# The second half's rows are normed beside units 8 to 10 instead of beside three recurrences

## The chip, the cores and the metric

The kernel runs on one core of a Trainium2 chip. What counts is the device time of one execution in microseconds (us). A profiled execution gives, beside its time, a record of every instruction on the engines PE (matrix products; PEld is its weight loads), DVE, ACT and POOL, and of SP, which issues most of the transfers (DMAs).

## The reference

One inference step of a decoder with two layers: 2048 prompt tokens and 8 x 4 sample tokens of width 1024. Layer 0 (even) has a gated recurrence (HGRN2) and attention with forgetting in parallel; layer 1 (odd) is a gated linear attention (GLA) with four heads. Each layer norms its input rows, multiplies them by an input matrix, mixes, gates, and adds the product with an output matrix to its input. Cut to the part that the change touches:

```
def run_trunk(x, ...):
    # layer 0
    x = x + even_mixer(rmsnorm(x, norm_even[0]), ...)
    # layer 1
    x = x + odd_mixer(rmsnorm(x, norm_odd[0]), ...)
    return rmsnorm(x, final_norm), ...

def odd_mixer(h, w_in, w_gate, b_gate, gla_gain, w_out, gla_s0):
    proj = h @ w_in
    q, k, v, g, r = _split(proj, [C_KEY_WIDTH, C_KEY_WIDTH, C_VAL_WIDTH, C_VAL_WIDTH, C_GATE_RANK])
    log_f = jax.nn.log_sigmoid((r @ w_gate + b_gate)) / GLA_GATE_NORMALIZER
    o, s = gated_linear_chunked(q, k, v, log_f, gla_s0)       # per head, 128 keys x 256 values
    o = head_rmsnorm(o, gla_gain) * jax.nn.silu(g)
    return o @ w_out, s
```

What the change moves is `rmsnorm(x, norm_odd[0])` for the second half of the prompt rows.

## The kernel before, in words

The prompt is worked on in two halves of 1024 tokens; the first half carries the 32 sample tokens as well. The normed, transposed input of a half lies in one tile, `act`, as a high and a low half-precision part, and every product with a weight matrix is made of three matmuls (`mm3`, L603 to L607). There is one `act` tile, so the second half's rows can go into it only when the first half's products are done.

The products come in *units*, numbered in one list: units 0 to 3 are the even layer's output projection of the first half, 4 to 7 that of the second; 8 to 19 are the odd layer's input projections of the first half, three for each head (v, then q and k, then the gate g); 20 to 31 the same for the second half; 32 to 39 the odd layer's output projections. `dense(a, b)` makes units a to b-1 and, beside each, starts the weight load of the unit three further on (L334, on SP) and the split of the weights of the unit two further on into two parts (L352 to L360, on ACT, DVE and POOL). A unit of v (`proj_tm`) goes through 8 groups of 128 rows and one of the samples, a unit of q and k or of g (`proj_fm`) through six pieces of 352 columns; each fills a PSUM bank of the tag "pj", of which there are three, and ACT (and DVE) empties it (L1884 for v, L1938 and L1943 for q and k, L662 to L664 for g).

A head's recurrence is `lin_attn`: products of q and k (`gd`, then the levels `gl`, L738) whose results are copied by mask (L684, L753), rescaling of q, k and the decay (L771 to L773), the samples' states (`stS`, L823 to L828), and the chunks' products (`st`, `o`). `recur(hf, h, a)` runs it beside units a to a+2.

Rows are normed by `norm_store` in one step per 128 rows: it loads the rows (L540, SP) from the array `x1d` into a tile `x1r`, squares and sums them (L546, ACT), makes the reciprocal root (L410 on DVE, L412 on POOL), multiplies by the gain (L548, POOL), writes the high part (L553, ACT) and the low part (L554, DVE), and stores both (L555, SP) in the array `xs`. A step norms one row tile and finishes the one before it. For the second half (`hf == 1`) the tiles are two buffers of the tag "yr"; the load of a step is one step ahead. In the code loads stand behind the last transposing DMA (`self.last_turn`, L538 to L540, order of issue only). `norm_fetch` brings `xs` into `act` with transposing DMAs (L574, SP).

The order of the work: `mux(a, ta, b, tb)` writes out two streams of steps so that each is at the same share of its cost (`ta`, `tb`). A step of `prep(1)` counts 1000, a group of a unit of v 2640, a piece of the other units 3592. What is written out is only the priority: a scheduler that runs a simulated timeline at build time (`schedule_with_timeline_sim=True`, L2192) puts the instructions of each engine in an order, which then is fixed. `issue_after` adds edges to it.

Of the kernel before, what the change touches and what calls it, by code (L numbers as in the profile page):

```python
# [76 lines left out]
def mux(a, ta, b, tb):  # L77

    pa = pb = 0.0
    la = lb = True  # L80
    while la or lb:
        if la and (not lb or pa * tb <= pb * ta):
            c = next(a, None)
            la = c is not None
            pa += c or 0
        else:
            c = next(b, None)
            lb = c is not None
            pb += c or 0
        if c:  # L90
            yield c
# [20 lines left out]
def drain(g):  # L112
    for _ in g:
        pass
# [11 lines left out]
class Kern:  # L126
# [1847 lines left out]
    def phase_odd(self):  # L1974
# [4 lines left out]
        with pool("act2", side="right") as ap, pool("w2", side="right") as w0, pool("yr2", side="right") as y0, \  # L1979
# [34 lines left out]
            def dense(a, b):  # L2014
                return self.staged(units, a, b)

            def recur(hf, h, a):
                return mux(lins[hf](h), LIN_O[hf], dense(a, a + 3), 66000.0)

            def three(hf, a):  # L2020
                for h in range(3):
                    yield from recur(hf, h, a + 3 * h)

            def fetched(u):
                units[u][0][0]()
                self.early.add(u)
# [57 lines left out]
            def prep(hf):  # L2084

                def tiles(c0):
                    p, tag = (wp, "v8") if hf == 0 and c0 // P % 2 else (wpool, "yr")
                    t = p.tile([P, KT, 256], F32, tag=tag, name=f"x1r{hf}{c0}").rearrange("p k t -> p (k t)")
                    return t[:, :D], t[:, D:].bitcast(F16).rearrange("p (x d) -> p x d", x=2)

                return self.norm_store(wp, hf, tiles, grow, 1 + (hf == 0))
# [1 line left out]
            drain(mux(prep(0), 11500.0, dense(4, 7), 63000.0))  # L2093
            self.norm_fetch(act, 0, dense(7, 8))
            fetched(11)
            drain(dense(8, 11))
            drain(mux(prep(1), 10000.0, three(0, 11), 240000.0))
            fetched(23)
            self.norm_fetch(act, 1)
            drain(recur(0, 3, 20))  # L2100
# [95 lines left out]
```

## Time and profile before

| | |
|---|---|
| median of three runs | 2337.07 us |
| lowest and highest of them | 2333.03 and 2337.43 us |
| the profiled execution | 2338.06 us |
| its span, first to last instruction | 2336.2 us |
| mean granted clock of PE in it | 0.991 |
| busy: PE, PEld, DVE, ACT, POOL | 96%, 69%, 62%, 46%, 33% of the span |

The profile's times are counted from the span's start. Units 8 to 10 lie from 1458 to 1528, the recurrences of heads 0, 1 and 2 of the first half from 1528 to 1619, to 1714 and to 1811. Busy time of a stretch, waits (who waited for whom, by the semaphore that came last), the chain of waits that ended last, and the instructions in order of time are views of the same trace. Durations of matmuls overlap, since they are pipelined.

### The profile page before, as it was taken

The page shows a single profiled execution, that of the slowest core. Times are in us where ns is not written, and L with a number is a line of the kernel's source. Part 1 is how long each engine was busy: PE and PEld are TensorE (multiplying, and loading weights), DVE is VectorE, ACT ScalarE, POOL GpSimd, SP SyncE. Part 2 cuts the span into 40 slices and gives each one's busy share as a digit, 9 for nine tenths or more (in the row PEclk, how much of TensorE's full clock was granted, in tenths as well). Part 3 has the DMA queues.
Part 4 walks back from the last instruction along what each step waited for, and adds up shares of the span by engine and source line. Part 5 has one row for each costly group of instructions (what it writes and reads, how often), then busy time and mean ns, then how long its engine had stood idle before and what let it go on. Part 6 is the DMA issues. An engine that isn't in the chain of part 4 may idle for free.

```text
span 2336.2 us, 58122 instructions
## 1 busy us (share of the span) xinstructions
PE 2250.3 (96%) x23060; PEld 1604.1 (69%) x23060; DVE 1448.0 (62%) x3313; ACT 1076.2 (46%) x2360; POOL 768.7 (33%) x818
## 2 busy tenths in 40 slices
PE   7999999999999989999999999999899999999998
PEld 5667667864655876665545888777677666666887
DVE  7766577537655748667767445366675655557554
ACT  6434344333333326555656543546545545545343
POOL 2333324112212214223335445144552432322232
PEclk9999999999999999999999999999999999999999
DMA  7232334765441278877882968523233431115554
GB/s 201 66 93 67 94 106 152 182 170 138 147 136 43 89 178 268 247 234 221 271 249 73 341 198 261 141 84 119 75 113 86 126 104 58 46 58 163 167 188 150
DMA packets 375665, 344.87 MB, mean 148 GB/s; under 512 B 107633, under 2 KB 322994, under 8 KB 375394
## 3 DMA queue, kind: packets, MB, share of 16 engines
q1 hardware_dynamic: 373250, 334.54, 47.8%
q0 software_dynamic: 2144, 6.62, 0.8%
q8 instruction: 181, 2.97, 0.5%
q14 instruction: 90, 0.74, 0.1%
HBM read 244.54 MB, written 79.63 MB: 139 GB/s over the span
## 4 chain that ended last, share of the span: by engine, by line
PE 78%; DVE 8%; DMA 4%; ACT 3%; issue 2%; POOL 2%; SPq 2%; POOLq 0%; DVEq 0%; ACTq 0%
PE pt_o L605 4%; PE pt_o L607 4%; PE pt_o L606 4%; PE pkt L1546 2%; PE pt L1427 2%; PE pt_Cv L605 2%; PE pt_Cv L606 2%; PE pt_Cv L607 2%; PE sc L1605 1%; PE pv L1684 1%; PE pf_Ag L607 1%; PE pf_Ag L606 1%; PE pf_Ag L605 1%; PE pf_Bq L607 1%; PE pf_Bq L606 1%
## 5 line engine op out<-in xcount | busy, mean ns | idle before, releaser
L605 PE MATMUL pt_o<-w_o,act 128*128 128x256 f16 x1024 | 279.7, 273 | 2.3 <-ACT sg1C L662 2.3
L607 PE MATMUL pt_o<-w_o,act 128*128 128x256 f16 x1024 | 279.6, 273 | 0.9 <-POOL act L1785 0.9
L606 PE MATMUL pt_o<-w_o,act 128*128 128x256 f16 x1024 | 279.6, 273 | 0.0
L605 PEld LDWEIGHTS <-act 128*128 128x128 f16 x2304 | 226.7, 98 | 37.4 <-issue 4.1
L606 PEld LDWEIGHTS <-act 128*128 128x128 f16 x2304 | 226.8, 98 | 32.9 <-issue 3.6
L607 PEld LDWEIGHTS <-act 128*128 128x128 f16 x2304 | 226.8, 98 | 31.4 <-issue 1.9
L606 PE MATMUL pt_Cv<-w_Cv,act 128*128 128x256 f16 (+1 forms) x512 | 141.3, 276 | 0.0
L605 PE MATMUL pt_Cv<-w_Cv,act 128*128 128x256 f16 (+1 forms) x512 | 141.3, 276 | 0.0
L607 PE MATMUL pt_Cv<-w_Cv,act 128*128 128x256 f16 (+1 forms) x512 | 141.2, 276 | 0.0
L772 POOL TENSOR_TENSOR kA<-kA,fA 128x512 f32<-128x512 f32 (+1 forms) x56 | 77.9, 1392 | 186.2 <-PE gl_A L738 140.2
L772 POOL TENSOR_TENSOR kC<-kC,fC 128x512 f32<-128x512 f32 (+1 forms) x56 | 83.9, 1498 | 153.9 <-PE gl_C L738 107.8
L1407 POOL TENSOR_SCALAR L<-L,nm 128x512 f32<-128x512 f32 (+3 forms) x160 | 99.5, 638 | 104.6 <-DVE nm L1403 44.5
L1399 ACT ACTIVATE L<-L,nm,kc 128x512 f32<-128x512 f32 (+3 forms) x160 | 118.2, 741 | 28.9 <-DVE nm L1397 27.6
L1434 ACT ACTIVATE th<-pt 128x512 f16<-128x512 f32 (+3 forms) x159 | 81.6, 528 | 85.1 <-PE pt L1427 82.0
L1435 DVE TENSOR_TENSOR tl<-pt,th 128x512 f16<-128x512 f32 (+3 forms) x159 | 95.0, 608 | 20.3 <-ACT th L1434 18.3
L1427 PE MATMUL pt<-ident,L 128*128 128x128 f32 x544 | 90.6, 278 | 2.1 <-DVE tl L1435 1.1
L1546 PEld LDWEIGHTS pkt<-ident,pgcache_fox_k 128*128 128x128 f32 x512 | 58.9, 142 | 42.9 <-issue 25.6
L1427 PEld LDWEIGHTS pt<-ident,L 128*128 128x128 f32 x544 | 66.4, 142 | 25.8 <-DVE tl L1435 6.2
L1884 ACT ACTIVATE vC<-pt_Cv,kc 128x512 f32<-128x512 f32 (+1 forms) x40 | 23.9, 598 | 130.4 <-PE pt_Cv L607 130.4
L1546 PE MATMUL pkt<-ident,pgcache_fox_k 128*128 128x128 f32 x512 | 77.6, 279 | 6.1 <-DMA pgcache_fox_k<-in_cache_fox_k 1.8
L1374 POOL TENSOR_TENSOR cm<-cb,caus 128x128 f32<-128x128 f32 x64 | 29.1, 456 | 132.1 <-DVE mx L1391 114.4
L605 PE MATMUL pt_Bk<-w_Bk,act 128*128 128x256 f16 x256 | 70.5, 276 | 2.1 <-DVE Bvs L1049 1.8
(959 smaller groups left out, 6750.7 us busy)
## 6 DMA issues: line engine op xcount, KB each, us to landing
pgcache_fox_k<-in_cache_fox_k SPq DMA_DIRECT2D x128, 256.0 KB, 4.2
pgcache_fox_v<-in_cache_fox_v SPq DMA_DIRECT2D x128, 256.0 KB, 4.0
yr<-yT SPq DMA_DIRECT2D x16, 1024.0 KB, 8.1
x1d<-xo SPq DMA_DIRECT2D x44, 256.0 KB, 3.9
wr_Aqf<-in_w_in_even SPq DMA_DIRECT2D x64, 128.0 KB, 3.2
wr_o<-in_w_out_even SPq DMA_DIRECT2D x32, 256.0 KB, 5.3
xo<-in_x_prompt SPq DMA_DIRECT2D x32, 256.0 KB, 5.3
wr_Cv<-in_w_in_odd SPq DMA_DIRECT2D x32, 256.0 KB, 4.0
```

What stands on the lines that cost most here:

```text
L605: nc.tensor.matmul(ps, lh[0], rh[0], start=first, stop=False)
L606: nc.tensor.matmul(ps, lh[0], rh[1], start=False, stop=False)
L607: return nc.tensor.matmul(ps, lh[1], rh[0], start=False, stop=last)
L772: nc.gpsimd.tensor_tensor(kv[:, :, 0], kv[:, :, 0], t1.to_broadcast([P, nb, w]), ALU.mult)
L1374: self.last_cm = nc.gpsimd.tensor_tensor(cm, cb[:, tb * P : (tb + 1) * P], caus, ALU.add)
L1399: self.last_exp = nc.scalar.activation(lt[:, :w], lt[:, :w], AF.Exp, bias=nm[:, 0:1], scale=ib, accum_out=nm[:, 2 + j : 3 + j])
L1407: nc.gpsimd.tensor_scalar(lt[:, :w], lt[:, :w], nm[:, 1:2], 2.0**14, ALU.mult, ALU.mult)
L1427: nc.tensor.transpose(pt[:, w : w + P], rows[b][s // 4][0][:, (s % 4) * P : (s % 4 + 1) * P], self.ident)
L1434: nc.scalar.activation(th[:, a:w], pt[:, a:w], AF.Copy),
L1435: nc.vector.tensor_tensor(tl[:, a:w], pt[:, a:w], th[:, a:w], ALU.subtract)))
L1546: last = nc.tensor.transpose(pk[:, j * P : (j + 1) * P], pgs[j][:, h * P : (h + 1) * P], self.ident)
L1884: r = nc.scalar.activation(v[h][:, g : g + cnt], ps[:, :, :256], AF.Copy, scale=c)
```

## The change

`prep(1)`, the norm of the second half's eight row tiles, is written out beside units 8 to 10 (`dense(8, 11)`), with the share of its steps set to 66000 of cost. Before, it was written out beside the recurrences of the heads 0, 1 and 2 with their units 11 to 19 (`three(0, 11)`), spread over 240000. Nothing else is different: the same instructions, tiles and transfers are made.

```
             drain(mux(prep(0), 11500.0, dense(4, 7), 63000.0))
             self.norm_fetch(act, 0, dense(7, 8))
             fetched(11)
-            drain(dense(8, 11))
-            drain(mux(prep(1), 10000.0, three(0, 11), 240000.0))
+            drain(mux(prep(1), 10000.0, dense(8, 11), 66000.0))
+            drain(three(0, 11))
             fetched(23)
             self.norm_fetch(act, 1)
             drain(recur(0, 3, 20))
```

More of the change, by code (lines that the diff above doesn't have):

```diff
@@ L2095, in phase_odd @@
             fetched(11)
-            drain(dense(8, 11))
-            drain(mux(prep(1), 10000.0, three(0, 11), 240000.0))
+            drain(mux(prep(1), 10000.0, dense(8, 11), 66000.0))
+            drain(three(0, 11))
             fetched(23)
```

## The prediction

> **What bounds the kernel now.** I read the page first, then busy time by stretch around the lines that change, then the waits of PE there, the chain of waits, and at last the queues of SP and ACT in order of time.
>
> ```profile
> span 2336.2 us, 58122 instructions
> ```
>
> The profiled execution took 2338.06 us: 1.86 us lie outside the span, which the change does not touch. It stands 1.0 us above the median of the three runs shown, 2337.07; sums are made on the profiled execution and the difference is put on the median. About 0.2%, 4.7 us, is what a measurement of this kernel can tell from no change.
>
> Four stretches, from the busy time by stretch (stretch; its length; then PE, weight load, DVE, ACT and POOL with busy us and instruction counts; PE clock; DMA share; GB/s). The first holds units 8 to 10, the three after it the recurrences of heads 0, 1 and 2:
>
> ```profile
> 1458.20:1528.30 70.10, 69.39 (x582) 49.42 (x579) 21.26 (x56) 35.28 (x62) 8.14 (x7) 1.00 0.51 130
> 1528.30:1619.10 90.80, 87.49 (x1073) 65.42 (x1062) 62.32 (x114) 49.27 (x108) 43.88 (x33) 1.00 0.33 104
> 1619.10:1714.40 95.30, 87.83 (x1000) 65.53 (x996) 64.77 (x116) 50.74 (x108) 46.73 (x35) 0.98 0.34 105
> 1714.40:1811.00 96.60, 95.38 (x1253) 72.50 (x1253) 62.47 (x124) 43.88 (x98) 37.13 (x30) 1.00 0.33 83
> ```
>
> PE is the bound in all four: its idle time is 0.7, 3.3, 7.5 and 1.2 us. So only PE's waits can be won or lost. They are named in the waits of PE (who waited, for whom, us, times, longest), in units 8 to 10, then at head 0:
>
> ```profile
> PE pf_C00k L605 <- DVE uC L1927: 0.6, 1, 0.6
> ```
>
> ```profile
> PE gl_C L738 <- issue: 1.4, 1, 1.4
> PE stS_C L823 <- DVE s_C L827: 1.3, 1, 1.3
> ```
>
> At head 1, then at head 2:
>
> ```profile
> PE gl_C L738 <- DVE qC L771: 2.7, 1, 2.7
> PE gl_C L738 <- issue: 1.8, 1, 1.8
> PE stS_C L823 <- DVE s_C L827: 1.8, 1, 1.8
> ```
>
> ```profile
> PE stS_C L823 <- DVE s_C L827: 1.1, 1, 1.1
> ```
>
> The waits of stS_C return in all three recurrences, with four, three and one row of the second half beside them (1.8, 1.3, 1.1): nearly all of that wait belongs to the recurrence. The 2.7 us stand in head 1's stretch alone. The chain of waits (start, us, what) passes there through the rows' own steps:
>
> ```profile
> 1627.72 2.37 POOL x1r L548
> 1630.09 1.51 POOL rsr_n L412
> 1631.62 1.16 ACT x1r L553
> ```
>
> Two rows were begun together; the second one's power on POOL and its copy on ACT came late, its split on DVE (L554) held the masked copies of the first level behind it, and PE stood until 1636.92. The clock followed:
>
> ```profile
> 1637.51:1640.92 3.41, 3.41 (x34) 2.44 (x23) 3.09 (x8) 0.00 (x0) 1.97 (x2) 0.50 0.30 118
> ```
>
> 3.41 us at half the granted clock are 1.7 us lost.
>
> **Part A, what is taken out of the recurrences.** 2.7 + 1.7 = 4.4 us, if no two rows meet there any more. Head 1's stretch also waits 0.4 us longer at gl_C and 0.5 us longer at stS_C than head 0's, so the upper end is 5.3; the lower end is 0, if the stall only moves. I take 4.4, the part that the chain itself puts on the rows.
>
> **Part B, what is added to units 8 to 10.** Eight rows, each with a load and a store on SP, two passes on ACT, a multiplication and a power on POOL, a split on DVE. Durations and landings where they run now, from the tile's and the lines' instructions (count; min/median/max; the landings are of the load L540 and then of the store L555):
>
> ```profile
> L546 ACT ACTIVATE nsq<-x1r x8: 1042/1048/1057, 1530.9 to 1717.6; 128x1024 bf16<-128x1024 f32 x8
> L548 POOL TENSOR_TENSOR x1r<-x1r,grow x8: 2362/2370/2590, 1532.1 to 1718.8; 128x1024 f32<-128x1024 f32 x8
> L553 ACT ACTIVATE x1r<-x1r,rsr_n x8: 1133/1148/1149, 1537.1 to 1723.8; 128x1024 f16<-128x1024 f32 x8
> L554 DVE SCALAR_TENSOR_TENSOR x1r<-x1r,rsr_n x8: 1275/1283/2202, 1538.3 to 1724.9; 128x1024 f16<-128x1024 f32 x8
> L412 POOL TENSOR_TENSOR rsr_n<-rst_n,mhalf x8: 567/1190/1823, 1535.2 to 1722.0; 128x1 f32<-128x1 f32 x8
> DMA to landing us min/median/max: 3.7/4.1/4.7
> DMA to landing us min/median/max: 2.6/3.1/5.4
> ```
>
> As sums of busy time this fits: DVE 21.3 + 8 x 1.28 = 31.5 of 70.1 us, POOL 8.1 + 8 x (2.37 + 1.19) = 36.6, ACT 35.3 + 8 x (1.05 + 1.15) = 52.9; the first two stay hidden. ACT is the engine to look at, because it empties PE's banks here (three of them, tag "pj") and works through its queue in a fixed order: where an instruction early in that order waits for a transfer, the evacuations behind it wait too. Its waits in this stretch now; then, in the recurrences, for the rows' power; then in the stretch of units 4 to 7, where the first half's nine rows are normed:
>
> ```profile
> ACT wr_Cv L358 <- DMA wr_Cv<-in_w_in_odd: 3.8, 2, 2.4
> ACT wr_Cqk L358 <- DMA wr_Cqk<-in_w_in_odd: 2.5, 2, 1.2
> ACT wr_Cg L358 <- DMA wr_Cg<-in_w_in_odd: 1.3, 2, 0.8
> ```
>
> ```profile
> ACT x1r L553 <- POOL rsr_n L412: 7.7, 5, 2.5
> ```
>
> ```profile
> ACT x1r L553 <- POOL rsr_n L412: 15.0, 7, 3.9
> ACT nsq L546 <- DMA x1r<-x1d: 6.9, 5, 3.8
> ```
>
> ACT's account of the 70.1 us then is 52.9 busy, 7.6 of the waits that are there already, 7.7 to 15.0 for the power, 0 to 6.9 for the loads: 68.2 to 82.4 us. It overruns by -1.9 to 12.3 us. That such a wait reaches PE in this very stretch is seen now, after a wait for weights (ACT in order of time, first two evacuations as they run undisturbed):
>
> ```profile
> 1463.95 0.47 ACT L1884 ACTIVATE vC<-pt_Cv,kc 128x256 f32<-128x256 f32 x1 [2.31 <-PE pt_Cv L607]
> 1466.73 0.47 ACT L1884 ACTIVATE vC<-pt_Cv,kc 128x256 f32<-128x256 f32 x1 [2.31 <-PE pt_Cv L607]
> ```
>
> ```profile
> 1494.17 0.72 ACT L358 ACTIVATE wr_Cv<-wr_Cv,kc 128x512 f32<-128x512 f32 x1 [2.44 <-DMA wr_Cv<-in_w_in_odd]
> 1496.24 0.72 ACT L358 ACTIVATE wr_Cv<-wr_Cv,kc 128x512 f32<-128x512 f32 x1 [1.34 <-DMA wr_Cv<-in_w_in_odd]
> 1496.86 0.54 ACT L1938 ACTIVATE qC<-pf_C00q,kc 128x352 f32<-128x352 f32 x1
> ```
>
> The two waits delay qC to 1496.86, and PE's 0.6 us above are what comes of it.
>
> The place where it bites is the first row. Its load is written behind the last transposing DMA of the first half (line 539), and SP is not through with those before 1472.75 (SP in order of time, then the landing of the two loads at that place):
>
> ```profile
> 1464.93 7.82 SPq L574 DMA_TRANSPOSE act<-xs  x3
> 1472.86 4.11 SPq L334 DMA_DIRECT2D wr_Cqk<-in_w_in_odd  x8
> 1477.06 0.89 SPq L540 DMA_DIRECT2D x1r<-x1d  x2
> ```
>
> ```profile
> DMA to landing us min/median/max: 5.7/6.1/6.6
> ```
>
> So row 0 lands at about 1472.8 + 6.1 = 1478.9. In the code written out it is normed after three groups of unit 8 (one step per 6600 of cost, 2640 a group), that is behind the evacuation at 1466.73. If the order on ACT keeps that place, the fourth group's evacuation, due at 1469.5, comes at 1478.9 + 1.05 and ends at 1480.4; PE needs that bank for its seventh group at 1466.73 + 3 x 2.78 = 1475.1, and stands 5.3 us. At the other end, with the row behind the sixth group's evacuation or later, it costs nothing. The loads now stand on SP ahead of where they were written (the code has them behind unit 10), so the order is not simply the written one; but an order fixed before the run that knew the true end of the transposes would be luck. I take 5.3.
>
> Later rows: two buffers ("yr"), so a row's load waits until the store two rows back has landed. One round is 4.1 + 1.05 + 2.37 + 1.19 + 1.15 + 1.28 + 3.1 = 14.2 us, four rounds from 1478.9 would last until 1536, 8 us past the stretch; the account above leaves 12.3 - 5.3 = 7.0 us as the most that these rows can add, 0 as the least. I take 3.0, a little under the middle, because PE is by then already late and the rows come nearer to their places. The 5.3-us wait brings the half clock once, 1.7. Part B is 5.3 + 3.0 + 1.7 = 10.0 us.
>
> [...]
>
> **Part C, the queues that are passed.** The two first loads move ahead of the eight weight loads at 1472.86, 0.89 us of SP; these weights are for unit 12, some 50 us later, so it is hidden. Stores wait on SP for DVE's split, and the weights of unit 14 (the wr_Cv above, for which ACT waits already) may stand behind one: 0 to 2 us, inside the account's range. Nothing is won behind the recurrences: the first half's columns are read until unit 19, beside head 2's recurrence, and the second half's transposes wait for that, not for the rows.
>
> **Sum.** -4.4 + 10.0 = +5.6 us: 2343.7 for the profiled execution, 2342.7 on the median.
>
> **The rivals.**
>
> One, not slower: the order puts row 0 behind the sixth group's evacuation and the rest into ACT's gaps (2.3 us before each evacuation above). Then only part A counts, -4.4 to -5.3: 2332.7 to 2331.8. For it: 17 us of ACT are idle in the sum of busy time; against it: 7.6 us of that are waits for transfers which already reach PE once. It decides from the sixth group on.
>
> Two, its extension: DVE was held up by POOL's multiplications in the recurrences and is freed, so that every wait that DVE ended goes: 2.7 + 1.8 + 1.3 + 1.1 + 1.7 = 8.6 us, 2328.5. The rows speak against it: DVE is busy 62.5 us in head 2's stretch with one row, and 62.3 in head 0's with three. [...]
>
> Three, the stall moves: rows 6 and 7 end at about 1536 and meet at the head of head 0's recurrence as two do now at head 1's, with nothing lost in units 8 to 10. Then -4.4 + 4.4 = 0, 2337.1.
>
> Four, the order of the engines does not follow the written place, and the rows stay beside the recurrences: 0, 2337.1.
>
> **How the numbers follow.** Forecast 0.60, of which 0.05 end within 0.2% (part B under 9.1). Rival one 0.17, half of it past 4.7 us; two 0.05; three 0.13; four 0.05. Slower 0.55; within 0.2% 0.05 + 0.09 + 0.18 = 0.32; faster 0.08 + 0.05 = 0.13. The upper end is the account's 12.3 us and two half clocks, 3.4, with nothing won: +15.7, 2352; the lower end is rival one's, 2332; about 0.1 lies outside at each. The slower case alone spans 2338 to 2352.
>
> **What would show it.** Right: in units 8 to 10 a wait of 4 to 7 us of PE at the unit of v, ended by ACT, with ACT waiting for x1r's load just before; half clock behind it; the 2.7 us gone from head 1. Wrong: PE's idle time in units 8 to 10 still under 2 us, or the stall of two rows at head 0 instead, or rows whose squares still stand beside the recurrences.

## The result and the profile after

| | before | after |
|---|---|---|
| median of 6 runs each, taken in turn | 2335.05 us | 2351.41 us |
| lowest and highest | 2330.44 and 2343.57 | 2349.01 and 2355.01 |
| the profiled execution | 2338.06 us | 2353.72 us |

The ratio is 1.0071 with a 95% interval of 1.0056 to 1.0086: the change costs 16.6 us (13 to 20). The forecast was slower by 5.6 us, 2342.7, with a range that ended at 2352. The direction came as forecast, the loss is three times the sum, and the median lies just inside the upper end.

The page of after, first lines:

```profile
span 2351.9 us, 58120 instructions
...
PE 2249.2 (96%) x23060; PEld 1602.6 (68%) x23060; DVE 1446.3 (61%) x3313; ACT 1076.0 (46%) x2360; POOL 764.8 (33%) x818
```

PE is busy for 2249.2 us, against 2250.3 before: over the whole span the loss is idle time, and inside the stretches below half clock has its part. Where it lies is read from busy time by stretch, cut at the first product of units 8, 9, 10, 12 and 15 (stretch; length; PE, weight load, DVE, ACT, POOL with busy us and counts; PE clock; DMA share; GB/s). After:

```profile
1457.63:1496.32 38.69, 26.16 (x224) 20.50 (x222) 14.60 (x33) 10.73 (x19) 9.30 (x7) 0.82 0.84 205
1496.32:1528.30 31.98, 25.66 (x175) 15.72 (x173) 14.69 (x26) 21.34 (x37) 16.36 (x9) 0.89 0.41 137
1528.30:1579.68 51.38, 50.12 (x696) 37.54 (x690) 33.70 (x53) 26.83 (x44) 25.50 (x20) 1.00 0.35 110
1579.68:1669.62 89.94, 87.17 (x1065) 65.41 (x1061) 54.03 (x109) 43.32 (x97) 31.86 (x28) 1.00 0.24 72
```

Before, cut at the same products:

```profile
1458.19:1482.23 24.04, 24.04 (x225) 19.93 (x222) 7.58 (x33) 7.74 (x16) 3.04 (x3) 1.00 0.97 228
1482.23:1506.13 23.90, 23.19 (x162) 14.92 (x159) 7.03 (x17) 15.06 (x27) 2.33 (x2) 1.00 0.26 86
1506.13:1557.67 51.54, 50.27 (x705) 37.67 (x702) 31.19 (x50) 22.35 (x38) 23.30 (x16) 1.00 0.25 75
1557.67:1653.76 96.09, 89.38 (x1064) 66.35 (x1061) 64.46 (x116) 51.33 (x109) 46.65 (x36) 0.98 0.35 111
```

Unit 8 is longer by 14.65 us, unit 9 by 8.08; units 10 and 11 differ by -0.16; units 12 to 14, with head 1's stall of before in them, are shorter by 6.15. The sum is +16.4. The waits of PE beside units 8 to 10 (who waited, for whom, us, times, longest):

```profile
PE prT L1899 <- DVE rT L1900: 13.6, 2, 12.5
PE zC L1924 <- ACT kC L1943: 5.1, 1, 5.1
```

and the same view beside the recurrences, from 1545 to 1780; no gl_C waits for DVE's qC any more:

```profile
PE stS_C L823 <- DVE s_C L827: 3.6, 3, 1.3
PE gl_C L738 <- issue: 3.2, 2, 1.9
...
```

**The 12.5 us.** ACT in order of time:

```profile
1460.62 0.47 ACT L1884 ACTIVATE vC<-pt_Cv,kc 128x256 f32<-128x256 f32 x1 [19.13 <-PE pt_Cv L607]
1477.58 1.06 ACT L546 ACTIVATE nsq<-x1r 128x1024 bf16<-128x1024 f32 x1 [16.49 <-DMA x1r<-x1d]
...
1478.63 0.46 ACT L1884 ACTIVATE vC<-pt_Cv,kc 128x256 f32<-128x256 f32 x1
```

Row 0's square stands behind the first evacuation of unit 8, not behind the third, and waits 16.49 us for its load. In all, ACT waits for rows' loads beside units 8 to 10 (waits of ACT):

```profile
ACT nsq L546 <- DMA x1r<-x1d: 21.3, 3, 16.5
```

SP, in order of time, is busy with the transposing DMAs until 1472.3 and issues the load only then:

```profile
1452.38 19.91 SPq L574 DMA_TRANSPOSE act<-xs  x7
1472.38 1.15 SPq L540 DMA_DIRECT2D x1r<-x1d  x2
```

PE's wait ends on DVE, where row 0's root (L410) waits for the same square, ahead of the second group's gate columns (L1893 to L1895), for which PE waits. DVE in order of time:

```profile
1461.39 0.19 DVE L1894 COPY rt<-rh 128x64 f32<-128x64 f32 x1
1478.76 0.15 DVE L410 TENSOR_SCALAR rst_n<-nss 128x1 f32<-128x1 f32 x1 [17.03 <-ACT nsq L546]
1479.12 0.24 DVE L1893 TENSOR_SCALAR rh<-pt_Cv,kc 128x16 fp32r<-128x16 f32 x1 [0.21 <-ACT vC L1884]
1479.39 1.82 DVE L1894 COPY rt<-rh 128x64 f32<-128x64 f32 x1
```

The root's place costs nothing by itself: L1893 behind it waits another 0.21 us for ACT's evacuation. The copy that takes 0.19 us alone takes 1.82 here. It ends at 1481.21, when POOL's multiplication of row 0 has just ended (POOL in order of time, with a later piece that matters below):

```profile
1478.82 2.34 POOL L548 TENSOR_TENSOR x1r<-x1r,grow 128x1024 f32<-128x1024 f32 x1 [19.21 <-ACT nsq L546]
1506.45 6.04 POOL L360 TENSOR_TENSOR w_Cv<-wr_Cv,w_Cv 128x512 f16<-128x512 f32 x2
```

PE runs on at 1481.67. So 1.63 us at the end of PE's longest wait, 1.82 less 0.19, are the copy's. It ran long beside the multiplication; why, the trace does not show.

**The 5.1 us.** The chain of waits (start, us, what) shows how the first rows' lateness returns at unit 9:

```profile
1488.55 2.97 DMA xs<-x1r
1491.58 5.33 DMA x1r<-x1d
...
1506.48 4.45 POOL w_Cv L360
1510.93 0.22 issue
1511.16 1.35 POOL w_Cv L360
...
1512.52 0.38 SPq L334
...
1514.04 6.06 DMA x1r<-x1d
...
1521.08 0.19 ACT nsq L546
1521.27 0.44 ACT kC L1943
```

Row 2's load waits for row 0's store, since there are two buffers. POOL's split of unit 11's weights, 6.04 us for two instructions, leaves their buffer only at 1512.5; SP, which stands there with unit 14's weights, issues row 4's load behind them at 1514.04; ACT waits for both, 4.57 and 2.68 us for the weights and 0.56 for the row, and empties PE's bank only at 1521.2.

**The clock** is at half in two stretches:

```profile
1471.40:1485.05 13.65, 3.38 (x15) 2.28 (x16) 6.01 (x11) 7.47 (x14) 6.18 (x5) 0.50 0.72 195
1519.20:1526.03 6.83, 4.22 (x25) 2.29 (x26) 1.35 (x3) 4.19 (x7) 2.86 (x2) 0.50 0.51 179
```

In the first of them products of 272 columns start 0.227 us apart, behind it 0.116. PE worked for 3.38 and 4.22 us of the two, so 1.7 and 2.1 us are lost.

### The profile page after: what moved, and what is told of

Read it like the earlier page. It is cut to its first block, busy times and chain, and to the rows that moved or that the text cites. A ratio compares the mean times of both kernels' runs of the same rounds, so it can differ in the third digit from the quotient of the medians.

```text
span 2351.9 us, 58120 instructions
## 1 busy us (share of the span) xinstructions
PE 2249.2 (96%) x23060; PEld 1602.6 (68%) x23060; DVE 1446.3 (61%) x3313; ACT 1076.0 (46%) x2360; POOL 764.8 (33%) x818
## 4 chain that ended last, share of the span: by engine, by line
PE 76%; DVE 9%; DMA 5%; ACT 3%; issue 3%; POOL 2%; SPq 1%; POOLq 0%; DVEq 0%; ACTq 0%
PE pt_o L605 4%; PE pt_o L607 4%; PE pt_o L606 4%; PE pkt L1546 2%; PE pt L1427 2%; PE pt_Cv L605 2%; PE pt_Cv L606 2%; PE pt_Cv L607 2%; PE sc L1605 1%; PE pv L1684 1%; PE pf_Ag L607 1%; PE pf_Ag L606 1%; PE pf_Ag L605 1%; PE pf_Bq L606 1%; PE pf_Bq L605 1%
## 5 line engine op out<-in xcount | busy, mean ns | idle before, releaser
L1427 PEld LDWEIGHTS pt<-ident,L 128*128 128x128 f32 x544 | 66.9, 143 | 25.6 <-DVE tl L1435 6.0
L1884 ACT ACTIVATE vC<-pt_Cv,kc 128x512 f32<-128x512 f32 (+1 forms) x40 | 23.9, 598 | 125.5 <-PE pt_Cv L607 125.5
```

The costliest lines, as they stand in the source:

```text
L1427: nc.tensor.transpose(pt[:, w : w + P], rows[b][s // 4][0][:, (s % 4) * P : (s % 4 + 1) * P], self.ident)
L1884: r = nc.scalar.activation(v[h][:, g : g + cnt], ps[:, :, :256], AF.Copy, scale=c)
```

## The experiments

All times are medians beside runs of the kernel before on the same chip; ratios are to it, with 95% intervals. The question was first whether the place of the squares in the engines' order makes the loss (order theory) or the amount of work beside these units (account theory).

**Rows from unit 9 on.**

```
-            drain(mux(prep(1), 10000.0, dense(8, 11), 66000.0))
+            drain(dense(8, 9))
+            drain(mux(prep(1), 10000.0, dense(9, 11), 44000.0))
```

> Unit 8 runs alone; all eight rows are written out beside units 9 and 10 (44000 of cost), the rest as after the change. Order theory (the loss is row 0's square on ACT, put behind the first evacuation of unit 8 while its load waits behind the transposing DMAs: 12.5 us of PE and 1.7 of half clock; a second stall of 5.1 and 2.1 us comes from unit 14's weights behind the rows' stores on SP): row 0's square now stands behind the last evacuation of unit 8, due at about 1485, its load lands at about 1479, so 14.2 us go; the second stall may stay or go: before -5 to +4 us, and no wait of PE over 2 us in unit 8. Account theory (eight rows are too much work for ACT beside these units, wherever they stand): the same work in 46 us in place of 70, so a loss of 16 us or more, spread over units 9 and 10.

Measured: 2342.08 against 2333.51 us, 1.0038 (1.0022 to 1.0055). Unit 8 takes 25.8 us: the 12.5-us wait is gone. Six of the eight squares now stand beside units 9 and 10, and these units are longer by 1.7 and 2.0 us. That is against the account theory. But the time, +8.9 us, lies outside the -5 to +4 of the order theory too: the largest part is a new wait at head 0 (waits of PE):

```profile
PE gl_C L738 <- DVE qC L692: 7.9, 1, 7.9
...
PE pf_C00k L605 <- DVE uC L1927: 2.6, 1, 2.6
```

DVE in order of time there, and then POOL:

```profile
1544.04 1.27 DVE L554 SCALAR_TENSOR_TENSOR x1r<-x1r,rsr_n 128x1024 f16<-128x1024 f32 x1
1545.47 2.88 DVE L664 SCALAR_TENSOR_TENSOR sg1C<-th_C,sg1C 128x352 f32<-128x352 f32 x2
1548.59 1.24 DVE L692 TENSOR_TENSOR qC<-qC,fC 128x1056 f32<-128x1056 f32 x1
```

```profile
1545.19 2.35 POOL L548 TENSOR_TENSOR x1r<-x1r,grow 128x1024 f32<-128x1024 f32 x1 [2.28 <-ACT nsq L546]
```

The last two rows meet head 0's beginning: row 6's split and row 7's multiplication, beside which two instructions of the gate take 2.88 us in place of twice 0.51, stand ahead of the rescaling (L692) that PE waits for. This is the prediction's third rival; it came about in this kernel, not in the one predicted, and unit 11, in which it lies, is 10.9 us longer, not 4.4.

**Loads not held behind the transposing DMAs.**

```
-                if self.last_turn is not None:
+                if self.last_turn is not None and hf == 0:
```

> As after the change, but the loads of the second half's rows are not held behind the last transposing DMA of the first half. The squares stay early on ACT (rows 0 and 1 ahead of unit 8's first evacuation); only their loads come some 15 us sooner. Order theory: the 12.5-us wait of PE and its half clock are gone, the first transposes may be late by up to 3 us; with the second stall (7.2 us) kept +2 to +6 us against before, without it -5 to 0. Account theory: the same work in the same stretch, so the loss stays at +10 to +16 us.

Measured: 2349.59 against 2333.51 us, 1.0064 (1.0039 to 1.0089), +14.9 us, so the order theory's range failed. The order on SP is fixed too, and it put the two loads between the third and the fourth transposing DMA (SP, then the waits of ACT):

```profile
1450.58 6.17 SPq L574 DMA_TRANSPOSE act<-xs  x2
1456.84 1.00 SPq L540 DMA_DIRECT2D x1r<-x1d  x2
1457.94 14.82 SPq L574 DMA_TRANSPOSE act<-xs  x5
1472.85 1.01 SPq L555 DMA_DIRECT2D xs<-x1r  x2
```

```profile
ACT nsq L546 <- DMA x1r<-x1d: 37.3, 5, 21.8
```

On ACT rows 0 and 1 stood ahead of the first evacuation here, with squares and copies, and ended at 1470.2; rows 0 and 1 were stored at 1472.85, behind all the transposing DMAs, so row 2 was late again. The account theory had the number, but ACT stood 37.3 us waiting for loads: not work but waiting filled it.

**Only row 0 beside unit 8.**

```
-            drain(mux(prep(1), 10000.0, dense(8, 11), 66000.0))
-            drain(three(0, 11))
+            rows = prep(1)
+            drain(mux(islice(rows, 2), 10000.0, dense(8, 11), 66000.0))
+            drain(mux(rows, 10000.0, three(0, 11), 240000.0))
```

> Only the loads of rows 0 and 1 and the square of row 0 are written out beside unit 8, as after the change; rows 1 to 7 stay beside the recurrences. Order theory: one row is enough for the first stall, PE waits 11 to 13 us at unit 8 and 1.7 are lost to half clock; units 9 and 10 run as before; head 1's 4.4 us may stay or go: +9 to +15 us. Account theory: one row adds 2.2 us to ACT, which has 17 us idle there: 0 to +3 us.

Measured: 2347.18 against 2333.51 us, 1.0054 (1.0036 to 1.0072). The waits of PE, units 8 to 14:

```profile
PE prT L1900 <- DVE rT L1901: 11.9, 1, 11.9
...
PE gl_C L739 <- DVE qC L772: 3.2, 2, 2.7
```

One row makes the whole first stall: unit 8 takes 38.9 us, against 38.7 after the change, where two squares stand in it; unit 9 takes 22.8. Head 1 keeps its 2.7 us. So one row's first step (square, root and multiplication) by itself brings +12.6 us, with nothing won behind it.

**Rows not normed, two ways.** The first trial copied normed rows in DRAM in place of the norm; the second leaves the norm out whole and lets the second half's transposing DMAs fetch the first half's rows. The edit of the second, against the kernel before, in two pieces:

```
-            dc = T if c0 >= HALF else hf * HALF + c0
+            dc = T if c0 >= HALF else c0
             self.last_turn = self.nc.sync.dma_start_transpose(
...
             drain(dense(8, 11))
-            drain(mux(prep(1), 10000.0, three(0, 11), 240000.0))
+            drain(three(0, 11))
```

> The second half's rows are not normed at all; eight transfers copy the first half's normed rows to their place, so ACT, DVE and POOL lose this work and the transposes still have their data. It prices the part taken out of the recurrences. If the 2.7 us of head 1 with its half clock belong to the rows: -4.4 to -5.3 us against before. If they belong to the recurrence: 0. If DVE was held up by POOL's multiplications in all three recurrences: -8 or more.

> The norm of the second half's rows is left out whole (no loads, no work, no stores), and the second half's transposing DMAs fetch the first half's normed rows. The first trial of this kind copied rows in DRAM, and its copies held up unit 11's weights (9.1 us of PE at unit 9), so its time says nothing; its heads 0 to 2 waited 8.7 us against 12.5. Without the copies: -4.4 to -5.5 us against before, if the 2.7 us of head 1 and their half clock are all that the rows cost; 0 if the rows cost nothing; -8 or more if POOL's multiplications hold DVE up in all three recurrences.

Measured: 2338.97 against 2333.51 us (1.0020, 1.0005 to 1.0034) for the first, where PE waited 9.1 us in unit 9, as ACT waited 11.0 us for weights whose load stood behind the copies (wr_Cg, unit 13's, not unit 11's as the second expectation has it); it says nothing of the norm. The second: 2329.13 against 2334.73 us, 0.9975 (0.9961 to 0.9988), that is -5.8 us (-9.1 to -2.8). Its waits of PE in units 8 to 14:

```profile
PE stS_C L823 <- DVE s_C L827: 3.7, 3, 1.3
...
```

So the rows beside the recurrences cost what part A said, 4.4 to 5.3, or a little more; and the waits of stS_C, still 3.7 us with no row there, are the recurrence's own. That is against the second rival, which had them go.

**Loads and stores on POOL's queue.**

```
-                if self.last_turn is not None:
+                if self.last_turn is not None and hf == 0:
...
-                nc.sync.dma_start(fly[x][0], self.x1d[dc : dc + n])
+                (nc.gpsimd if hf else nc.sync).dma_start(fly[x][0], self.x1d[dc : dc + n])
```

and the store of L555 likewise.

> As after the change, but the second half's rows are loaded and stored on POOL's queue in place of SP's, and not held behind the transposing DMAs. The run with only the hold taken away still had ACT wait 37.3 us for these loads, since SP itself is busy with the transposing DMAs until 1472.8. Order theory (ACT's fixed order waits for loads that come late): rows 0 and 1 now land before the first evacuation of unit 8, so the 12.5-us wait and its half clock are gone; ACT's waits for these loads fall under 10 us in all; against before -4 to +6 us, the upper end if POOL, which now waits for DVE's splits ahead of each store, comes late with the weights. Account theory (ACT, DVE and POOL have too much work in this stretch wherever the loads are): +10 to +16 us as after the change.

Measured: 2351.81 against 2334.73 us, 1.0080 (1.0056 to 1.0103), +18.7 us: above the ranges of both theories. In its trace the first two loads are early, and their squares stand ahead of unit 8's evacuations. But the transposing DMAs beside them are slow (SP in order of time; then the waits of PE):

```profile
1447.08 34.25 SPq L574 DMA_TRANSPOSE act<-xs  x7
```

```profile
PE pt_Cv L605 <- DMA act<-xs: 8.3, 4, 5.1
```

34.25 us in place of 19.91, and PE waits for the columns themselves. ACT still waited 34.7 us for loads, where under 10 was expected: row 2's load on POOL's queue stood 6.4 us behind a transposing DMA, and its square waited 9.98. The profiled run, 2343.89 us, is the fastest of the six, so the trace shows half of the loss; where the other half lies stays open.

**Without POOL's multiplication.** As after the change, and in `norm_store`:

```
-            nc.gpsimd.tensor_tensor(xt, xt, gain[:n], ALU.mult)
+            if hf == 0:
+                nc.gpsimd.tensor_tensor(xt, xt, gain[:n], ALU.mult)
```

> As after the change, but POOL's multiplication of the second half's rows by the gain is left out. The first stall (12.5 us and 1.7 of half clock) should stay by every theory. The second one (PE 5.1 us and 2.1 of half clock at unit 9): POOL theory (POOL's multiplication and DVE's two-input instructions stretch each other, a split of 1.15 us on POOL took 4.75, so unit 11's raw weights come free late and unit 14's load is issued at 1512.5): it falls under 1.5 us, and the time is +8 to +11 us against before. Queue theory (unit 14's weights stand behind the rows' stores on SP): 4 to 6 us stay, +13 to +17 us.

Measured: 2346.23 against 2334.73 us, 1.0047 (1.0032 to 1.0062), +11.0. The first stall stays (11.1 us), DVE's copy behind it takes 0.20 us again, and the second falls to 2.2, with full clock:

```profile
PE prT L1900 <- DVE rT L1901: 11.1, 1, 11.1
PE pf_C00g L606 <- ACT kC L1944: 2.2, 1, 2.2
```

The time is at the upper end of the POOL theory's range; the rest of the second stall, 2.2 us where it said under 1.5, is ACT's wait for a row's load, 3.9 us. The multiplication is also 2.4 us of each row's own chain, so this run doesn't part the longer copies and splits beside it from its own share of that chain.

**Attempts at a better version**, with the rows beside the recurrences: spread wider; multiplied on DVE; then both.

```
-            drain(mux(prep(1), 10000.0, three(0, 11), 240000.0))
+            drain(mux(prep(1), 10000.0, three(0, 11), 310000.0))
```

```
-            nc.gpsimd.tensor_tensor(xt, xt, gain[:n], ALU.mult)
+            if hf == 0:
+                nc.gpsimd.tensor_tensor(xt, xt, gain[:n], ALU.mult)
+            else:
+                nc.vector.tensor_tensor(xt, xt, gain[:n], ALU.mult)
```

> As before the change, the rows beside the recurrences, but spread over 310000 of cost in place of 240000, so that no two squares stand next to each other on ACT (before: two at head 1). If head 1's stall is the meeting of two rows: no wait of gl_C over 1.9 us at head 1, -3 to -5 us against before. If one row is enough, or the stall moves to another head: -1 to +2 us.

> As before the change, but the second half's rows are multiplied by the gain on DVE in place of POOL (2.37 us a row on POOL, about 1.28 on DVE by the split of the same rows). POOL theory (POOL's long multiplication makes the rows come late and stretches DVE's instructions beside it, and so causes head 1's stall): no wait of gl_C over 1.9 us at head 1, -3 to -6 us against before, the floor being the run without rows (-5.8). Rival (DVE, busy 62 of 91 to 97 us in each recurrence, is the engine that the masked copies wait for, and gets 10 us more): 0 to +6 us.

> Both: the rows beside the recurrences, spread over 310000 of cost, and multiplied on DVE. The spread alone measured 0 to +0.26% and lost 2.6 us and 6.8 us of half clock at unit 15, where ACT had waited for POOL and for weights. If that came through POOL's multiplication, this is the best of the four with the rows in it: -3 to -6 us against before. If DVE becomes the bound: 0 to +6 us.

Measured: 2337.58 against 2334.73 us, 1.0013 (1.0000 to 1.0026); 2331.33 against 2332.54, 0.9995 (0.9985 to 1.0006); 2335.60 against 2332.54, 1.0006 (0.9996 to 1.0016). None won the 3 us or more that the first theory of each expectation asked for. Each took the stall out of units 12 to 14 and found one in units 15 to 17, as the table shows (us from the first product of a unit to that of the next column's, in the profiled executions):

| kernel | unit 8 | 9 | 10, 11 | 12 to 14 | 15 to 17 |
|---|---|---|---|---|---|
| before | 24.0 | 23.9 | 51.5 | 96.1 | 90.6 |
| after | 38.7 | 32.0 | 51.4 | 89.9 | 90.8 |
| rows from unit 9 on | 25.8 | 25.6 | 64.4 | 89.5 | 90.6 |
| loads not held | 40.5 | 24.4 | 52.8 | 90.4 | 90.5 |
| only row 0 beside unit 8 | 38.9 | 22.8 | 52.0 | 95.8 | 90.3 |
| on POOL's queue | 36.1 | 22.8 | 56.4 | 89.9 | 90.7 |
| not normed (second way) | 24.4 | 22.8 | 51.5 | 90.7 | 91.1 |
| no multiplication | 38.4 | 25.4 | 51.4 | 90.7 | 90.4 |
| spread 310000 | 24.0 | 22.8 | 51.5 | 90.5 | 95.5 |
| on DVE, 240000 | 24.0 | 26.2 | 51.5 | 90.4 | 93.3 |
| on DVE, 310000 | 24.0 | 23.6 | 51.5 | 90.6 | 95.2 |

With the multiplication on DVE and the spread of before, two squares still stand side by side near head 1's beginning (at 1617.4 and 1618.6 us), and its stall is gone all the same: the meeting of two rows alone does not make it, POOL's multiplication has a part. No kernel that norms the rows is measurably faster than the kernel before.

## Why the prediction was right in direction and short in size

- **Part A, -4.4:** held. The 2.7 us and their half clock are gone, units 12 to 14 measure -6.2, the run without the norm -5.8 in all.
- **Part B, first-row stall, 5.3:** the term that was mis-sized; it measured 12.5. The mechanism was the one named (the load behind the transposing DMAs; it landed by 1477.6 against 1478.9 forecast). The place was wrong: I took the written place, behind the third evacuation, and the order had the square behind the first. The same working gives it: with the second group's bank held, PE stands from the end of group 4, 1458.2 + 4 x 2.78 = 1469.3 (it stood from 1469.1), to 1480.4, which is 11.1 us; DVE's copy behind POOL adds 1.6, which makes 12.7. The prediction had in hand that the order is not simply the written one, but took a place as late as the written one or later, never earlier, so its account of ACT (at most 12.3 us for all rows) was not an upper bound: it had at most 6.9 us for the loads, and ACT waited 21.3.
- **Who ends it:** forecast was ACT alone. The square on ACT set 11.1 us of it, as the run without POOL's multiplication shows; the last part is DVE's copy, held beside that multiplication.
- **Part B, later rows, 3.0:** measured 1.0 + 5.1 - 0.6 (the wait of before that is gone) = 5.5, inside its 0 to 7.0. The two buffers and the late weights of unit 14 that it named are in the chain; that POOL's split of unit 11's weights holds them was not seen.
- **Half clock, 1.7:** two stretches, 1.7 + 2.1.
- **Sum by these terms:** -6.2 + 12.5 + 5.5 + 3.8 = +15.6, against +15.7 in the spans.
- **The range:** that the median lies inside it is luck. Its upper end, +15.7, was made of 12.3 + 3.4 with nothing won; measured were 18.0 + 3.8 with 6.2 won, and the two errors cancel. (+15.7 on the median is 2352.8, which was put down as 2352.)
- **Part C:** the passed weights of unit 12 cost nothing, as said; the 0 to 2 us for unit 14's went into the later rows.
- **Rivals:** one fell with the first evacuation; DVE was held beside POOL's multiplication as two has it (0.19 us became 1.82, and stayed 0.20 without the multiplication), but the price that two puts on it is not there (stS_C waits without rows); three appeared once the rows started at unit 9; four fell, the squares ran from 1477.6 to 1546.1. The last two of the eight, from 1536.9 on, still stand beside head 0's recurrence, as the four rounds reckoned to 1536 implied, and PE waits for no row there.

## What to carry to other kernels

When work is moved beside another stretch, ask of its first instruction on every engine whose order is fixed what it waits for and when that arrives, and price every place that it may get in the order, those ahead of the written one too: a square of 1.06 us, two evacuations too early and waiting for its load, cost 12.5 us, with 1.6 of a stretched copy in it. Removing one order rule did not help here, where SP, which issues the loads, was busy with transposing DMAs until 1472.8; and a stall taken out of one head can come back at the next, so price a version by stretches before believing the one that improved.

## What the runs showed of the hardware

- A small copy on DVE (L1894, 0.19 us alone) took 1.82 and 2.27 us after the change, from 1479.39 and 1481.79, beside POOL's multiplications of rows 0 and 1 (2.34 and 2.35 us, from 1478.82 and 1481.66); without the multiplication it took 0.20. A split of weights on POOL (L360, 1.15 us at its shortest before the change) took 4.75 there, from 1506.45, while DVE split weights (L353) and rows (L554); without the multiplication the two splits of unit 11's weights took 1.16 and 2.40.
- Transposing DMAs that took 19.9 us for seven after the change took 34.3 with loads and stores of rows running beside them on POOL's queue; their median landing rose from 6.8 to 11.5 us.
- Half clock came in stretches of 3.41 us (before, at 1637.51) and multiples (6.83 and 13.65 after, at 1519.20 and 1471.40; these two starts lie 47.80 us apart, 14 x 3.414). The length of PE's wait does not settle by itself whether it comes. With POOL's queue a wait of 2.02 us ended at 1526.35, and half clock stands behind it (the first line below); with rows from unit 9 on one of 2.60 us ended at 1500.47, and the clock stays full (the second line):

```profile
1526.40:1529.81 3.41, 3.41 (x13) 1.72 (x13) 2.93 (x4) 3.31 (x6) 1.16 (x2) 0.51 0.87 227
```

```profile
1500.47:1503.88 3.41, 3.41 (x23) 2.24 (x23) 0.58 (x1) 1.61 (x3) 0.00 (x0) 1.00 0.94 205
```

What does settle it was not tested.
